# An output stage of seven products for all pairs, with every engine's operations placed on one clock

## The chip, the cores and the metric

The kernel runs on one core of one Trainium2 chip. Its engines are TensorE (PE), VectorE (DVE), ScalarE (ACT), GpSimd (POOL) and SyncE (SP), each with an instruction stream of its own that is worked off in order; they wait for each other by semaphores. The metric is the device time of one execution in microseconds (us). Before the change the median of three runs is 1524.33 us (1519.32 to 1524.88).

## The reference

One step of a hybrid decoder layer in fp32, for a prompt of 4096 tokens and 64 sample tokens with a width of 1024:

```python
h = _rmsnorm(x, g_pre)
z = h @ w_in
cb, cc, ch, cg, q, k, v, ag, mq, mg = _split_cols(z)
...
out_a = jax.nn.silu(cg) * cb * conv
...
out_b = jax.nn.silu(ag) * o_b
...
out_c = jax.nn.silu(mg) * o_c
y = jnp.concatenate([out_a, out_b, out_c], axis=-1) @ w_out
return x + _rmsnorm(y, g_post), new_conv, new_k, new_v
```

`out_a` is a gated short convolution (256 columns); `o_b` is attention over a sliding window of 128 keys with 8 query heads on 2 key heads (512 columns); `o_c` is attention of 4 heads over 256 memory tokens (256 columns). The softmax of the window has one more term per head, exp(sink - m), in its denominator, and m is the maximum over the scores and the sink.

## The kernel before

A product of two fp32 matrices is made of three matmuls on TensorE: both operands are split into a high and a low part (a cast and a subtraction), and high x high, low x high and high x low are added up in PSUM. A matrix of 2x2 blocks can be multiplied with seven block products instead of eight, at the price of sums of blocks ahead and combinations behind; the input projection does this for nearly all of its blocks (its matmuls are line 368, its evictions line 375).

The kernel has two parts. The input projection goes over blocks of 520 tokens in three phases and writes queries and keys (`qd`), values (`vd`) and the gated mix (`md`) to DRAM. Then comes the output stage, in 16 pairs (`c`) of two blocks of 128 tokens. For each pair it does two halves (`h`) of attention and one output projection, and TensorE's stream interleaves them: the small matmuls of a half stand between groups of output matmuls.

One half of attention consists of these steps: the window scores (`ws`, line 1333), copied to `sm` by ScalarE (line 1342) and masked by VectorE (`COPY_PREDICATED`); maximum, exponentials with their sums (line 1289), the sink's share (`wes`, line 1286, added to `wden`, line 1294), the multiplication by the reciprocal `wrd` (line 1297); transposes (`wt`), a copy to `wpt` (line 1307) and two selections by GpSimd (lines 1312 and 1315). Beside them the memory scores (`xs`, line 1355), exponentials (`xp`, line 1180), multiplication by the reciprocal `xrd` and 0.5 (line 1192, GpSimd, the "factors"), transposes (`xt`, line 1368) and a copy back (line 1369). Then come the products with the values (`wo`, lines 1390, 1396 and 1059) and the gates, which write into the pair's `place`.

The output projection of a pair is a product of 256 tokens x 1024 by 1024 x 1024. The first three pairs (`Block.run`, line 1639) do it plainly: 96 matmuls of 512 columns. The other thirteen (`Pair.run`, line 1750) use seven products for the k tiles 0 to 3 and plain matmuls for the k tiles 4 to 7: 90. The weights are kept on the chip in 16 split tiles `wo`, and the sums of weights (T1, T3, T4, T6, T7) are built during the first three pairs. The sums of the mix are made by GpSimd (line 1695), split by ScalarE and VectorE (lines 1678 and 1681); the products collect in four PSUM banks, `c12`, `c21`, `c11` and `c22`, and are combined by VectorE by way of the buffers `s3` and `s4` (lines 1770 to 1800). Each finished half row is multiplied by the gain (`gpost`), squared and summed (line 1753); from the sums comes a factor (`yst`, lines 1654 and 1655, the power on GpSimd), and the "residual" xr = y * factor + x (line 1660, 1024 columns) is stored.

The order of TensorE in the output stage is that of the program: a table of places (`what`, filled by `at`) calls the parts of attention and sums between the products. VectorE, ScalarE, GpSimd and SP are ordered by a scheduler, with a number of pinned instructions.

Of the kernel before, what the change touches and what calls it, by code (L numbers as in the profile page):

```python
# [52 lines left out]
def hybrid_layer(ctx: ExitStack, tc: tile.TileContext, a: dict):  # L53
# [23 lines left out]
    qd = tc.dram_tile([2, 7, P, NT], F32R, name="qd")  # L77
    vd = tc.dram_tile([P, NT], F32, name="vd")
# [22 lines left out]
    def open_phase(ph):  # L101
# [3 lines left out]
        if ph == 0:  # L105
            z = [z_pool(kept_z, f"z{n}") for n in range(4)]
            natp = own.enter_context(tc.tile_pool(name="nat", bufs=2))
            zp[2] = [*z, z_pool(own, "z4")]
            kept_z.z4 = zp[2][-1]
        elif ph == 1:  # L110
            zp[2].remove(kept_z.z4)
            zp[2][:0] = [z_pool(own, f"z{n}") for n in (5, 6, 7)]
        else:

            tp = [own.enter_context(tc.tile_pool(name=f"t2{n}", bufs=3)) for n in "ab"]
            z = [z_pool(own, n) for n in ("z8", "z9", "y0", "y1", "z10", "y2")]
            zp[2], zp[1] = [z[0], z[1], z[4]], [z[2], z[3], z[5]]
# [281 lines left out]
    def finish_parts(b, z, idx, second):  # L399

        z = flat(z)
        if idx == 0 and b == NBLK - 1:
            kl = temp("kl")
            S.copy(kl[:, :P], z[:, 2 * HW - P :])
            store(a["o_kp"], kl[:, :P])
        hi = temp(f"zh{b}_{idx}", second)[:, : 2 * HW].bitcast(F32R)
        S.copy(hi, z)  # L407
        lo = (temp("kl_")[:, : 2 * HW] if idx == 0 else z).bitcast(F32R)
# [315 lines left out]
    def third_start():  # L724
# [8 lines left out]
        negs = third["negs"] = keep.tile([P, 2, P], F32, name="negs")  # L733
        tc.keep_in_program_order(DMA.dma_start(sink, a["sinks"].partition_broadcast(P)))
        V.tensor_scalar(nsink, sink, -1.0, None, op0=ALU.mult)
        tc.keep_in_program_order(DMA.dma_start(negs, a["wmask"]))
        G.tensor_copy(wmask, negs)  # L737
# [6 lines left out]
        third["mem"] = mem_stack.enter_context(tc.tile_pool(name="mem", bufs=3, side="right"))  # L744
        tc.keep_in_program_order(DMA.dma_start(gmem, a["gmem"]))
# [142 lines left out]
    wo, wo_raw = [[None, None] for _ in range(KT)], {}  # L888

    def wo_load(j):  # L890
        h, k = divmod(j, KT)
        if 10 <= j < 14:

            if j % 2 == 0:
                third["raw"] = hxp.tile([P, KH, HW], F32, tag="hx", name=f"wor{j}").rearrange("p k n -> p (k n)")
            wo_raw[j] = third["raw"][:, 512 * (j % 2) : 512 * (j % 2) + 512]
        else:
            wo_raw[j] = third["work"].tile([P, 512], F32, tag="u", name=f"wor{j}")
        DMA.dma_start(wo_raw[j], a["w_out"][k][:, 512 * h : 512 * h + 512])

    def wo_split(j):
        h, k = divmod(j, KT)
        wo[k][h] = wa.tile([P, 2, 512], F32R, tag="w", name=f"wo{k}_{h}")
        w_split(wo[k][h], wo_raw.pop(j))
# [16 lines left out]
    def input_projection():  # L921
        for i, (ph, b, p) in enumerate(steps):
# [32 lines left out]
            if i > 0 and steps[i - 1][0] == 1 and steps[i - 1][1] == NBLK - 1:  # L955

                o = PRODUCTS[steps[i - 1][2]][0]
                for q in range(len(PHASES[2])):
# [5 lines left out]
                    else:  # L964
                        jobs.append(load)
                        pending.setdefault(i + 1, []).append(fill)
            if ph == 2 and b == last:
                for j in ((0, 1, 2), (3, 4), (5, 6, 7), (8, 9, 10, 11), (12, 13, 14, 15), (), ())[p]:
                    jobs.append(lambda j=j: wo_load(j))
                    pending.setdefault(i + (3 if j in (10, 11) else 2), []).append(lambda j=j: wo_split(j))  # L970
                if p == 1:
                    pending.setdefault(i + 1, []).append(gains_load)
                if p == 4:
                    jobs.append(blocks[0].split)
# [36 lines left out]
    def open_attention():  # L1011

        nonlocal ps, mixp, places, vp, bp, yp, wt, sums
# [9 lines left out]
        wt = att.enter_context(tc.tile_pool(name="wt", bufs=6))  # L1023
        places = {tag: att.enter_context(tc.tile_pool(name=tag, bufs=1 if tag == "p" else 2)) for tag in ("sm", "p", "yn", "pt", "pv")}
        sums = {tag: att.enter_context(tc.tile_pool(name=tag, bufs=1)) for tag in ("s3", "s4", "sum")}
        bp = {"k": att.enter_context(tc.tile_pool(name="keys", bufs=1)), "vT": att.enter_context(tc.tile_pool(name="vT", bufs=1))}
        mixp = att.enter_context(tc.tile_pool(name="mixp", bufs=1))
        late = att.enter_context(tc.tile_pool(name="late", bufs=1))
# [4 lines left out]
    ps = mixp = places = vp = bp = yp = wt = sums = None  # L1033
# [27 lines left out]
    left = []  # L1061

    def finish_block(queued=False):

        while left:
            left.pop(0)(queued)

    class Chunk:


        def __init__(self, c):
            self.c, self.rds, self.q, self.ks = c, {}, [None, None], [None, None]
# [3 lines left out]
        def load_values(self):  # L1076
            pool = third["pre"] if self.c == 0 or self.c % 2 else bp["vT"]
            self.vT = pool.tile([P, CT], F32, tag="vT", name=f"vT{self.c}")
            DMA.dma_start(self.vT, vd[:, self.ts])

        def load_all_keys(self):

            self.kst = third["pre"].tile([P, 4, P + CT], F32R, tag="k", name="kst0")
# [10 lines left out]
        def load_keys(self, i):  # L1094

            t = self.t0 + i * P
            pool = bp["k"] if i else third["pre"]
            self.ks[i] = pool.tile([P, 4, P + CT] if i == 0 else [P, 4, CT], F32R, tag="k", name=f"kst{self.c}_{i}")[:, :, :CT]
            self.fill_keys(G if self.c == 1 else DMA, self.ks[i], t - P, CT)
# [157 lines left out]
        def window_unit(self, i, kvh, steps):  # L1257
# [4 lines left out]
            for half in range(2):  # L1262
# [7 lines left out]
                V.copy_predicated(sm[:, 2 * half : 2 * half + 2, :], third["wmask"], third["negs"] if first else s3[:, :, 0:P])  # L1270
# [860 lines left out]
```

## Time and profile before

| | us |
|---|---|
| median of the runs | 1524.33 |
| span of the profiled execution | 1517.9 |
| input projection (0 to 928.70) | 928.70 |
| first three pairs | 114.10 |
| next twelve pairs, 35.4 each | 424.60 |
| last pair, with the sample tokens' | 40.80 |
| after the last matmul | 9.70 |

The profile is of one execution, whose span lies 6.4 us below the median. A row of groups gives the line, the engine, the operation, out<-in by the program's names, the shapes, the count, the busy time with the mean in ns of one, and the idle time of the engine ahead of them with what ended it. Matmuls overlap: a matmul of 512 columns is shown with about 395 ns, while the next one starts some 230 ns after it. So the price of a matmul is read from the starts in the timeline.

### The profile page before, as it was taken

Reading aid. Unit: us, or ns where it says so; the run is one execution under the profiler, and the core shown is the slowest. Engines: PE = TensorE matmul, PEld = TensorE weight load, DVE = VectorE, ACT = ScalarE, POOL = GpSimd, SP = SyncE. Lnnn points to the kernel's source line nnn. Section 1 sums busy time; section 2 is a strip of 40 time slices with the busy share of each in tenths; the row PEclk is TensorE's granted clock in tenths of the full one; section 3 lists DMA queues with packets and bytes.
Section 4 is the critical chain, followed back from the end, with each engine's and each line's share of the span. In section 5 each row is a group of like instructions: output and inputs, shape, how many; then the busy total and the mean of one; then the engine's idle time right before and its main releaser. Section 6 shows DMA issues by size and latency. Waiting matters only on the chain.

```text
span 1517.9 us, 30946 instructions
## 1 busy us (share of the span) xinstructions
PE 1500.6 (99%) x11497; PEld 1378.7 (91%) x11497; DVE 1199.3 (79%) x2089; ACT 842.7 (56%) x2066; POOL 392.7 (26%) x576
## 2 busy tenths in 40 slices
PE   9999999999999999999999999999999999999997
PEld 9999999999999999999999999788888788877875
DVE  6779888899988777897777768777877788878874
ACT  6676666475322222354454536666666666666652
POOL 0223222211300000000201301234455544455641
PEclk9999999999999999999999999999999999999999
DMA  9999999878855333578786697989755565666552
GB/s 258 157 265 221 289 294 271 264 246 298 211 183 183 128 116 125 180 235 292 227 265 238 208 307 252 282 238 238 201 168 157 160 164 162 176 174 169 153 201 70
DMA packets 217323, 319.71 MB, mean 211 GB/s; under 512 B 37398, under 2 KB 143382, under 8 KB 217142
## 3 DMA queue, kind: packets, MB, share of 16 engines
q1 hardware_dynamic: 196837, 273.54, 61.1%
q0 software_dynamic: 19616, 43.15, 10.5%
q8 instruction: 91, 1.49, 0.4%
q10 hardware_dynamic: 720, 1.05, 0.2%
q14 instruction: 59, 0.48, 0.1%
HBM read 208.50 MB, written 110.15 MB: 210 GB/s over the span
## 4 chain that ended last, share of the span: by engine, by line
PE 79%; DVE 8%; DMA 5%; ACT 4%; issue 2%; SPq 1%; POOL 0%; ACTq 0%; DVEq 0%; POOLq 0%
PE c L368 53%; PE y_c L1750 12%; PE y L1639 2%; PE ws L1333 2%; PE xt L1368 2%; ACT xp L1180 1%; DVE xr L1660 1%; DMA place<-in_xt 1%; PE wo L1059 1%; PE wo L1396 1%; DVE xmx L1169 1%; PE xs L1355 1%; DMA wr_3A<-in_w_in 1%; PE wt L1378 1%; DMA kst<-qd 1%
## 5 line engine op out<-in xcount | busy, mean ns | idle before, releaser
L375 DVE TENSOR_TENSOR z<-c,z 128x520 f32<-128x520 f32 (+1 forms) x308 | 194.3, 644 | 83.7 <-PE c L368 82.7
L1750 PE MATMUL y_c<-wo,pw 128*128 128x512 f32 (+1 forms) x636 | 158.9, 392 | 0.0
L1289 ACT ACTIVATE sm<-sm,wnm 128x128 f32<-128x128 f32 x256 | 99.4, 389 | 72.1 <-DVE wnm L1283 72.1
L1750 PEld LDWEIGHTS y_c<-wo,pw 128*128 128x128 f32 x636 | 114.0, 188 | 27.1 <-issue 3.7
L1192 POOL TENSOR_SCALAR xp<-xp,xrd 128x256 f32<-128x256 f32 x128 | 71.5, 575 | 191.2 <-DVE xrd L1186 186.7
L1180 ACT ACTIVATE xp<-xs,xnm 128x256 f32<-128x256 f32 x128 | 59.1, 473 | 31.5 <-DVE xnm L1170 22.9
L737 POOL CAST wmask<-negs 128x256 uint8<-128x256 f32 x1 | 1.2, 1162 | 266.7 <-DMA negs<-in_wmask 266.7
L1639 PE MATMUL y<-wo,mh 128*128 128x512 f32 x192 | 64.5, 398 | 0.2 <-ACT y L1648 0.2
L1312 POOL TENSOR_SCALAR_AFFINE_SELECT wpv<-wpt 128x512 f32<-128x512 f32 x62 | 56.8, 938 | 8.7 <-ACT wpt L1307 8.5
L1315 POOL TENSOR_SCALAR_AFFINE_SELECT wpt<-wpt 128x512 f32<-128x512 f32 x64 | 46.0, 737 | 38.6 <-ACT wpt L1307 38.2
L1333 PE MATMUL ws<-kst,q 128*128 128x256 f32 (+1 forms) x480 | 55.7, 297 | 0.0
L1343 DVE COPY_PREDICATED sm<-wmask,ws 128x512 f32<-128x512 uint8 x60 | 40.5, 729 | 19.0 <-ACT sm L1342 19.0
L1660 DVE SCALAR_TENSOR_TENSOR xr<-yn,yst,xr 128x1024 f32<-128x1024 f32 (+2 forms) x35 | 51.6, 1479 | 4.6 <-POOL yst L1655 4.5
L407 ACT CAST zh<-z 128x520 fp32r<-128x520 f32 x56 | 33.3, 624 | 35.3 <-DVE z L375 31.9
L276 ACT ACTIVATE nat<-nat 104x1024 f32<-104x1024 f32 x40 | 42.2, 1056 | 18.3 <-DMA nat<-in_x_p 18.3
L377 ACT COPY z<-c 128x520 f32<-128x520 f32 (+1 forms) x44 | 24.4, 554 | 49.3 <-PE c L368 45.0
L1333 PEld LDWEIGHTS ws<-kst,q 128*128 128x128 f32 (+1 forms) x480 | 46.4, 187 | 4.1
L1289 ACT ACTIVATION_READ_ACCUMULATOR sm<-sm,wnm 128x1 f32 x256 | 47.9, 187 | 0.0
L1297 DVE TENSOR_TENSOR sm<-sm,wrd 128x512 f32<-128x512 f32 x64 | 44.5, 695 | 1.1
L1750 PE MATMUL y_c<-wo,pc 128*128 128x512 f32 (+1 forms) x162 | 45.1, 400 | 0.0
L164 POOL DMA_DIRECT2D md<-th x48 | 26.2, 547 | 72.0 <-DVE th L425 59.5
L1639 PEld LDWEIGHTS y<-wo,mh 128*128 128x128 f32 x192 | 36.1, 188 | 8.9 <-issue 1.0
(1037 smaller groups left out, 5538.8 us busy)
## 6 DMA issues: line engine op xcount, KB each, us to landing
q<-qd SPq DMA_DIRECT2D x168, 128.0 KB
xr<-in_x_p SPq DMA_DIRECT2D x32, 512.0 KB
nat<-in_x_p SPq DMA_DIRECT2D x39, 416.0 KB
o_yp<-xr SPq DMA_DIRECT2D x31, 512.0 KB
kst<-qd SPq DMA_DIRECT2D x112, 128.0 KB
md<-th POOLq DMA_DIRECT2D x48, 260.0 KB, 6.4
qd<-zh SPq DMA_DIRECT2D x48, 260.0 KB
qd<-z SPq DMA_DIRECT2D x48, 260.0 KB
```

The costliest lines, as they stand in the source:

```text
L368: TE.matmul(bank[:, :HW], l, r, start=first and i == 0, stop=last and i == 3 * KH - 1)
L375: add = lambda dst, other: V.tensor_tensor(dst, c, other, op=ALU.add)
L1180: S.activation(p[:, i, :], s[:, i, :], AF.Exp, bias=nm[:, i : i + 1], scale=SCALE, accum_out=den[:, i : i + 1])
L1192: G.tensor_scalar(p[:, i, :], p[:, i, :], self.rds[h][:, i : i + 1], 0.5, op0=ALU.mult, op1=ALU.mult)
L1289: S.activation(sm[:, hh, :], sm[:, hh, :], AF.Exp, bias=nm[:, hh : hh + 1], scale=SCALE, accum_out=den[:, hh : hh + 1])
L1297: V.tensor_tensor(sm, sm, rd.unsqueeze(2).to_broadcast([P, 4, P]), op=ALU.mult)
L1312: G.affine_select(pv.rearrange("p (h q) -> p h q", h=4), p3, pattern=[[0, 4], [-1, P]], compare_op=ALU.is_gt, fill=0.0, base=0, channel_mu ...
L1315: G.affine_select(p3, p3, pattern=[[0, 4], [1, P]], compare_op=ALU.is_ge, fill=0.0, base=0, channel_multiplier=-1)
L1333: TE.matmul(out(kvh, col, bank), q(kvh, col, bank)[r], k(kvh, part)[r], start=first, stop=True, skip_group_check=not first, **place)
L1639: TE.matmul(acc, self.hl[l][:, k], wo[k][p][:, r], start=k + i == 0, stop=k + i == KT + 1)
L1660: x = V.scalar_tensor_tensor(self.xr[:m, cs], yn[:m, cs], st[:m, 3:4], self.xr[:m, cs], op0=ALU.mult, op1=ALU.add)
L1750: TE.matmul(acc, a[:, l, k], w[:, r, cs], start=first, stop=k == len(ws) - 1 and i == 2, skip_group_check=not new)
```

## The change

All 16 pairs now use seven products for the whole of the projection: the eight k tiles are put into two groups of four, (0, 1, 4, 5) and (2, 3, 6, 7), and each product has four k tiles, so a pair has 7 x 4 x 3 = 84 matmuls. The last of the products of the last pair stays in two quarters.

The weights follow. The sums T1, T3, T4, T6, T7 and the plain b11 are built and split by GpSimd during phase 1 of the input projection (21 tiles; 41 loads, 41 sums or differences, 21 casts, 42 stores to DRAM), and b22 and most of b11 late in phase 2. The fourth k tile of six operands has no place on the chip and is loaded again for each pair (`STREAMED`, six DMAs of 512 KB a pair on SP).

In the output stage all five engines now follow one table: each operation of attention, projection, loads and stores has a place in units of a period of 34.0 per pair, and the five streams are written in the order of the places. Besides, the factors move from GpSimd to ScalarE (their 0.5 goes into the copy behind the transposes); the sink becomes a 129th column of `sm`, so that the exponentials' sums hold it and `wes` and its addition go; the squares and gains of two half rows read PSUM, without a copy ahead; keys are kept in a ring of three blocks, which halves their loads; the raw projections of the sample tokens are kept in DRAM (`zd`).

```diff
+    G0, G1 = (0, 1, 4, 5), (2, 3, 6, 7)
+    STREAMED = (("T3", 3), ("T4", 3), ("b11", 3), ("T1", 3), ("T6", 3), ("T7", 3))
...
+    def out_sum(o, j):
+        x, y = out_raw.pop((o, j))
+        if o in WALKED:
+            G.tensor_tensor(x, x, y, op=ALU.subtract if o in ("T3", "T4") else ALU.add)
+        hi, lo = y.bitcast(F32R), x.bitcast(F32R)
+        G.tensor_copy(hi, x)
+        G.tensor_tensor(lo, x, f(hi), op=ALU.subtract)
+        G.dma_start(f(td[o, j][:, 0]), f(hi))
+        G.dma_start(f(td[o, j][:, 1]), f(lo))
...
+        def window_sink(self, i, kvh):
+            S.copy(self.sms[kvh][:, :, P:], third["nsink"][:, 4 * kvh : 4 * kvh + 4].unsqueeze(2))
...
+        def memory_factors(self, h, p):
+            for i in range(CT // P):
+                S.mul(p[:, i, :], p[:, i, :], self.rds[h][:, i : i + 1])
...
+    PERIOD = 34.0
...
+        SUMS = {"rows0": ((1, 0), (0, 0), ALU.add), "rows1": ((1, 1), (0, 1), ALU.add), "diag": ((1, 0), (0, 1), ALU.add),
+                "down0": ((1, 1), (1, 0), ALU.subtract), "down1": ((0, 0), (0, 1), ALU.subtract)}
...
+        def direct(self, n, p, bank):
+            S.activation(self.half(n, p), self.acc[bank], AF.Square, scale=float(D) ** -0.5, accum_out=self.st[n][:, p : p + 1])
...
+    ORDER = (("M1", "c12", "a11", "T3", True), ("M3", "c12", "rows0", "b22", False), ("M2", "c21", "a22", "T4", True),
+             ("M4", "c21", "rows1", "b11", False), ("M5", "c11", "diag", "T1", True), ("M7", "c11", "down1", "T7", False),
+             ("M6", "c22", "down0", "T6", True))
...
+                "s4": lambda: p.combine("s4", "s3", "c21", ALU.add), "y00": lambda: p.combine((0, 0), "s4", "c12", ALU.subtract),
```

**TensorE, early in the ninth pair (`y8`), around the transposes and scores of half 19.** `xt` and `ws` are the transposes and window scores of that half, `wo9` its products with the values, `y8_...` the output products. Before:

```order
L1750 MATMUL y8_c21_15831<-wo2_0_11644,pr8_15804 128x512 x3
L1750 MATMUL y8_c21_15831<-wo3_0_11688,pr8_15804 128x512 x3
L1750 MATMUL y8_c12_15830<-wo4_1_11863,pw0_8_15884 128x512 x3
...
L1750 MATMUL y8_c12_15830<-wo6_1_11882,pw0_8_15884 128x512 x3
L1750 MATMUL y8_c12_15830<-wo7_1_11885,pw0_8_15884 128x512 x3
L1368 MATMUL xt9_0_15932<-ident_63,xp9_0_15789 128x128 x8
L1333 MATMUL ws19_0_15942<-kst9_1_15633,q9_1_15638 128x256 x4
L1333 MATMUL ws19_1_15943<-kst9_1_15633,q9_1_15638 128x256 x4
...
L1390 MATMUL wo9_0_15962<-wpv18_0_15852,vt8_1_15378 64x256
...
L1059 MATMUL wo9_0_15962<-xp9_0_15789,mkv_8464 64x128 x8
L1750 MATMUL y8_c21_15831<-wo4_0_11691,pw1_8_15905 128x512 x3
```

After (`woT4` with `a228` is M2, `wob22` with `rows08` M3, `wob11` with `rows18` M4):

```order
L1660 MATMUL y8_c21_15947<-woT4_0_11938,a228_15878 128x512 x3
L1660 MATMUL y8_c21_15947<-woT4_1_11940,a228_15878 128x512 x3
L1660 MATMUL y8_c12_15894<-wob22_0_11847,rows08_15888 128x512 x3
L1660 MATMUL y8_c21_15947<-woT4_2_11973,a228_15878 128x512 x3
...
L1660 MATMUL y8_c12_15894<-wob22_3_11902,rows08_15888 128x512 x3
L1660 MATMUL y8_c21_15947<-woT4_3_15876,a228_15878 128x512 x3
L1431 MATMUL xt9_0_16050<-ident_63,xp9_0_15943 128x128 x8
L1366 MATMUL ws19_0_16064<-ring_10053,q9_1_15958 128x256 x4
L1366 MATMUL ws19_1_16065<-ring_10053,q9_1_15958 128x256 x4
...
L1660 MATMUL y8_c21_15947<-wob11_0_12015,rows18_15995 128x512 x3
```

Before, the products of `wo2_0` with `pr8` (the later M4) stood ahead of the transposes, the products with the values followed the scores, and the next output matmuls went on in `c21` with the window's part `pw1`. Now M2 into `c21` ends directly ahead of the transposes, and M4, into the same bank, begins directly behind the scores; the products with the values come behind it.

**VectorE at the same place.** `s4` is the combination that reads `c21`, `xr` the residuals of the pair before, `sm18` the shares of half 18. Before:

```order
L1770 TENSOR_TENSOR yn7_1_15363<-y7_c22_15668,s3_7_15366 128x512
...
L1654 TENSOR_SCALAR yst7_1_15365<-yst7_1_15365 128x1
L1776 TENSOR_TENSOR yn7_1_15363<-yn7_1_15363,gpost_11647 128x512
L1787 TENSOR_TENSOR s4_8_15829<-s3_8_15828,y8_c21_15831 128x512
L1681 TENSOR_TENSOR pw0_8_15884<-place_159,pw0_8_15884 128x512
L1790 TENSOR_TENSOR yn8_0_15824<-s4_8_15829,y8_c12_15830 128x512
L1660 SCALAR_TENSOR_TENSOR xr15_14977<-yn7_1_15363,yst7_1_15365,xr15_14977 128x1024
L1681 TENSOR_TENSOR pw1_8_15905<-place_159,pw1_8_15905 128x512
L1793 TENSOR_TENSOR s3_8_15828<-s4_8_15829,y8_c21_15831 128x512
L1681 TENSOR_TENSOR pd8_15915<-diag8_15916,pd8_15915 128x256
L1681 TENSOR_TENSOR pc8_15926<-yn8_1_15825,pc8_15926 128x512
L1343 COPY_PREDICATED sm19_0_15979<-wmask_8468,ws19_0_15942 128x512
```

After:

```order
L1401 RECIPROCAL wrd18_0_15970<-wden18_0_15863 128x4
L1403 TENSOR_TENSOR sm18_0_15822<-sm18_0_15822,wrd18_0_15970 128x4x128
L1599 TENSOR_SCALAR yst7_0_15588<-yst7_0_15588 128x1
L1685 TENSOR_TENSOR yn7_0_15587<-yn7_0_15587,gpost_12206 128x512
L1213 RECIPROCAL xrd9_1_15992<-xden9_1_15951 128x2
L1604 SCALAR_TENSOR_TENSOR xr15_15892<-yn7_1_15603,yst7_1_15604,xr15_15892 128x1024
L1647 TENSOR_TENSOR diag8_15979<-rdiag8_15874,diag8_15979 128x512
L1647 TENSOR_TENSOR rows18_15995<-rrows18_15913,rows18_15995 128x512
L1604 SCALAR_TENSOR_TENSOR xr14_15890<-yn7_0_15587,yst7_0_15588,xr14_15890 128x1024
L1695 TENSOR_TENSOR s4_8_16088<-s3_8_15938,y8_c21_15947 128x512
L1678 TENSOR_TENSOR yn8_0_16043<-y8_c12_15894,gpost_12206 128x512
L1695 TENSOR_TENSOR yn8_0_16043<-s4_8_16088,y8_c12_15894 128x512
```

The residual `xr14` of the pair before now stands directly ahead of `s4_8`, with a share, a gain, the other residual and two lows in front of it; before, `s4_8` stood behind a gain, and the nearer residual came after it.

**ScalarE around the exponentials of the memory scores, in the eighth pair.** Before (the factors are on GpSimd, line 1192):

```order
L1678 CAST pa8_15650<-place_159 128x256 x2
L1759 COPY yn7_1_15363<-y7_c21_15369 128x512
L1180 ACTIVATE xp8_1_15589,xden8_2_15590<-xs8_1_15572,xnm8_2_15582 128x256 x2
L1180 ACTIVATE xp8_1_15589,xden8_3_15593<-xs8_1_15572,xnm8_3_15586 128x256 x2
L1307 COPY wpt17_0_15623<-wt17_15614 128x512
L1307 COPY wpt17_1_15628<-wt17_15614 128x512
L1753 ACTIVATE s4_7_15367,yst7_1_15365<-yn7_1_15363 128x512
L1369 COPY xp8_1_15589<-xt8_1_15669 128x1024
```

After:

```order
L1207 ACTIVATE xp8_0_15488,xden8_0_15489<-xs8_0_15449,xnm8_0_15480 128x256 x2
L1207 ACTIVATE xp8_0_15488,xden8_1_15496<-xs8_0_15449,xnm8_1_15476 128x256 x2
L1643 CAST diag7_15524<-rdiag7_15419 128x512
L1643 CAST rows17_15539<-rrows17_15458 128x512
L1424 ACTIVATE xp8_0_15488<-xp8_0_15488,xrd8_1_15536 128x256 x2
L1424 ACTIVATE xp8_0_15488<-xp8_0_15488,xrd8_0_15513 128x256 x2
L1455 ACTIVATE vt8_0_15470<-vtp8_15472 128x128
L1455 ACTIVATE vt8_1_15471<-vtp8_15472 128x128
```

The four factors (`xp8_0<-xp8_0,xrd8`) stand on ScalarE behind two casts of the next products' parts and ahead of the copies `vt`; the copy `yn7_1<-y7_c21` is no longer there.

More of the change, by code (lines that the diff above doesn't have):

```diff
@@ L1011, in open_attention @@
     def open_attention():
-        nonlocal ps, mixp, places, vp, bp, yp, wt, sums
+        nonlocal ps, mixp, places, vp, yp, wt, sums
         own.close()
@@ L2011, in hybrid_layer @@
[L2011 to L2024 removed]
+    ctx.enter_context(tc.manual_schedule(engines={mybir.EngineType.PE, mybir.EngineType.DVE, mybir.EngineType.SP,
+                                                  mybir.EngineType.Activation, mybir.EngineType.Pool}))
@@ L2025, in hybrid_layer @@
+    extra("tokens", sample_tokens)
+    for bh in range(2):
+        plan_sample_memory(bh)
+    plan_sample_window()
+    for o in ("T4", "T3"):
+        extra(f"sample {o}", lambda o=o: out_load(o, 3))
+    plan_sample_out()
+    plan_end()
+    for _, _, fn in sorted(plan, key=lambda item: item[:2]):
+        fn()
     att.close()
```

1200 lines of the change are left out of this document (583 added, 617 removed), and 20 rows, old and new, of tables (EXTRA, FIRST_HALVES, HALF).

## The prediction

> **What bounds the kernel now.** I read the page first, then the busy time by stage, then what TensorE waits for, and last one pair of the output stage instruction by instruction. The page says that TensorE is busy 99% of the span and carries 79% of the chain that ended last:
>
> ```profile
> span 1517.9 us, 30946 instructions
> ...
> PE 1500.6 (99%) x11497; PEld 1378.7 (91%) x11497; DVE 1199.3 (79%) x2089; ACT 842.7 (56%) x2066; POOL 392.7 (26%) x576
> ...
> PE 79%; DVE 8%; DMA 5%; ACT 4%; issue 2%; SPq 1%; POOL 0%; ACTq 0%; DVEq 0%; POOLq 0%
> ```
>
> By stage (columns: length; busy time and count of TensorE, of its weight load, of VectorE, ScalarE and GpSimd; granted clock; DMA share; GB/s) the rows are the input projection, the first three pairs, the next twelve pairs, the last pair, and the tail:
>
> ```profile
> 0.00:928.70 928.70, 924.64 (x7676) 916.45 (x7677) 745.68 (x1060) 466.43 (x797) 133.88 (x213) 1.00 0.76 227
> 928.70:1042.80 114.10, 112.94 (x752) 92.03 (x751) 88.06 (x207) 74.58 (x254) 37.97 (x59) 1.00 0.94 265
> 1042.80:1467.40 424.60, 422.52 (x2825) 339.75 (x2824) 337.47 (x758) 284.51 (x968) 212.46 (x290) 1.00 0.61 171
> 1467.40:1508.20 40.80, 40.49 (x248) 30.50 (x246) 24.49 (x60) 16.67 (x45) 7.38 (x13) 1.00 0.42 134
> 1508.20:1517.90 9.70, 0.03 (x1) 0.00 (x0) 3.61 (x7) 0.51 (x2) 1.01 (x2) 0.69 0.27 81
> ```
>
> TensorE's idle time is 4.1 us of 928.7, 1.2 of 114.1, 2.1 of 424.6 and 9.7 in the tail, at a granted clock of 1.00 throughout. Its waits are small; the longest single one that the view names in the output stage is this (total, times, longest):
>
> ```profile
> PE xt L1368 <- POOL xp L1192: 0.6, 1, 0.6
> ```
>
> So in the output stage the time is the sum of matmuls, one behind the other. A removed matmul is a saved one as long as the other engines still deliver in time, and they have room: one steady pair (the fifth of the twelve) reads, in the same columns,
>
> ```profile
> 1188.55:1223.96 35.41, 35.28 (x237) 28.43 (x237) 28.42 (x65) 23.93 (x83) 17.43 (x24) 1.00 0.61 166
> ```
>
> which leaves VectorE 7.0 us, ScalarE 11.5 us and GpSimd 18.0 us of 35.41 free.
>
> **The matmuls removed.** By the order of the program, output matmuls of 512 columns go from 96 (first three pairs) or 90 (the others) to 84 a pair, and the last pair loses 12 of 256 columns: 3x12 + 12x6 + 6 = 114 of 512 columns. The price is in TensorE's timeline of that pair (start, length, names, count):
>
> ```profile
> 1188.55 3.08 PE L1750 MATMUL y_c<-wo,pr 128*128 128x512 f32 x12
> 1191.46 2.99 PE L1750 MATMUL y_c<-wo,pw 128*128 128x512 f32 x12
> 1194.30 1.03 PE L1368 MATMUL xt<-ident,xp 128*128 128x128 f32 x8
> 1195.09 1.85 PE L1333 MATMUL ws<-kst,q 128*128 128x256 f32 x16
> 1196.87 0.43 PE L1390 MATMUL wo<-wpv,vt 64*64 64x256 f32 x2
> ...
> 1199.35 1.66 PE L1750 MATMUL y_c<-wo,pw 128*128 128x512 f32 x6
> 1200.84 1.54 PE L1750 MATMUL y_c<-wtT,pd 128*128 128x512 f32 x6
> 1202.22 1.11 PE L1355 MATMUL xs<-mk,q 128*128 128x256 f32 x8
> ...
> 1206.82 2.89 PE L1750 MATMUL y_c<-wo,pw 128*128 128x512 f32 x12
> 1209.55 1.03 PE L1368 MATMUL xt<-ident,xp 128*128 128x128 f32 x8
> ```
>
> From start to start, twelve matmuls take 2.91, 2.84 and 2.73 us: 0.2275 to 0.2425 each. I take 0.235: 114 x 0.235 = **-26.8 us** (-25.9 to -27.6). The Trainium skill (TensorE: Matmul & The Clock Gate, Wait — 56ns, not 53.3ns?) puts back-to-back matmuls at N / 2.4 GHz plus about 2.5 ns, 215.7 ns at 512 columns; by it the term would be -24.6. The rows here are 5 to 12% longer than that, and the rows decide.
>
> **More group starts.** Six matmuls that follow small ones take 1.49 us (1199.35 to 1200.84), the six behind them 1.38: a start costs 0.11. By the order, a steady pair now has nine places at which output matmuls follow other matmuls, and seven before: 2 x 0.11 x 16 = **+3.5 us** (0 to 7).
>
> **ScalarE, VectorE, GpSimd in the new pair.** From the same pair (busy, mean ns of one):
>
> ```profile
> L1192 POOL TENSOR_SCALAR xp<-xp,xrd 128x256 f32<-128x256 f32 x8 | 4.5, 576 | 10.3 <-DVE xrd L1186 10.3
> L1678 ACT CAST pa<-place 128x256 fp32r<-128x256 f32 x2 | 0.7, 396 | 0.0
> L1678 ACT CAST pc<-yn 128x512 fp32r<-128x512 f32 x1 | 0.6, 621 | 0.0
> L1286 ACT ACTIVATE wes<-wes 128x4 f32<-128x4 f32 x4 | 0.7, 189 | 0.0
> L1759 ACT COPY yn<-y_c 128x512 f32<-128x512 f32 x2 | 1.2, 588 | 3.3 <-PE y_c L1750 3.3
> L1695 POOL TENSOR_TENSOR yn<-mix 128x512 f32<-128x512 f32 x1 | 1.5, 1452 | 0.0
> L1695 POOL TENSOR_TENSOR sum<-place 128x256 f32<-128x256 f32 x2 | 1.5, 736 | 7.4 <-ACT sm L1289 5.1 <-DVE wes L1285 2.4
> L1776 POOL TENSOR_TENSOR yn<-yn,gpost 128x512 f32<-128x512 f32 x1 | 1.3, 1276 | 0.3 <-ACT s L1753 0.3
> ```
>
> The eight factor multiplications of a pair leave GpSimd (-4.5) for ScalarE. No trace shows that operation on ScalarE; the cast of the same 128x256 is the nearest row, 0.396, and the bounds are 0.19 (a 4-column operation) and 0.62 (a 512-column one): +3.2 us (1.5 to 5.0). ScalarE also loses four wes (-0.7) and two copies of y_c (-1.2; the squares now read PSUM), gains four 4-column sink copies (+0.7) and some 768 cast columns (+0.9, at 0.621 for 512): 23.9 + 2.9 = 26.8 of 34. GpSimd trades four 256-wide sums (2.9) for four 512-wide ones (5.8) and gives a gain back to VectorE (-1.3): 17.4 - 4.5 + 2.9 - 1.3 = 14.5. VectorE keeps about 28 less the wes and wden operations. All three fit beside some 34 us of matmuls, so what is left is the order: each waits in line.
>
> **The new tight place.** The order of the places puts one VectorE addition, s4, directly in front of TensorE: it must be done before the products of b11 write the same bank (called M4 here), and s4 itself waits for the products of T4 (M2). Between M2's end and M4 stand one set of transposes and one of scores, 1196.87 - 1194.30 = 2.57 us by the timeline. Directly ahead of s4 VectorE has the residual of the pair before; behind s4 wait a gain, y00 and the next half's mask. The rows:
>
> ```profile
> L1660 DVE SCALAR_TENSOR_TENSOR xr<-yn,yst,xr 128x1024 f32<-128x1024 f32 x2 | 3.4, 1704 | 0.0
> L1787 DVE TENSOR_TENSOR s<-s,y_c 128x512 f32<-128x512 f32 x1 | 0.7, 675 | 0.0
> L1766 DVE TENSOR_TENSOR yn<-yn,gpost 128x512 f32<-128x512 f32 x2 | 1.6, 798 | 1.4 <-ACT s L1753 1.4
> L1297 DVE TENSOR_TENSOR sm<-sm,wrd 128x512 f32<-128x512 f32 x4 | 2.8, 689 | 0.1
> ```
>
> If the residual begins as M2 ends, 1.70 + 0.68 = 2.38 us stand against 2.57: 0.2 us of slack, and VectorE arrives there behind a queue that holds two shares (0.69 each), a gain (0.80), the other residual (1.70) and two lows (as wide as a share; 0.69 each is my estimate). A second place is the transposes of the even half: they wait for the last factor on ScalarE, which stands behind the xexp and two casts there; on GpSimd four factors took 2.3 us, on ScalarE they should take about 1.6. I take 0.12 us per pair for both places together, **+2 us** (0 to 16, one us a pair).
>
> **Streamed weights.** Six tiles of 512 KB are now loaded again in each pair on SP's queue, among the queries, keys and stores. Each is issued behind the last products of its tile's predecessor, and SP waits there; queued behind it are the next half's queries and keys. The key loads halve (eight of 128 KB to 64 KB). The pair now moves 166 GB/s x 35.41 us = 5.9 MB at a share of 0.61; with 3.1 more and 0.5 less it is 8.5 MB in 34 us, 250 GB/s. The first three pairs ran at 265 GB/s and a share of 0.94 with TensorE busy 112.94 of 114.10, so the volume fits; I take **0** (0 to 16).
>
> **Stage start and input projection.** Before, the output stage began with twelve output matmuls (2.7 us by the price above), which covered the last evictions; the first scores now stand there and need them. The eviction of 512 columns is 0.69 (row below), and the first products wait for a softmax. I take **+2 us** (0 to 5). In phase 1 GpSimd gets 41 sums of 512 columns (1.452 each: 59.5 us) and 21 casts, where it had nearly nothing, and 41 loads. The phase has VectorE busy 745.68 of 928.70. Its most frequent group takes the same time where GpSimd is busy 78 of 290 us (first rows) and where it is busy 15 of 320:
>
> ```profile
> 40.00:330.00 290.00, 288.06 (x2416) 287.06 (x2415) 240.65 (x314) 184.60 (x333) 78.44 (x126) 1.00 0.96 256
> 380.00:700.00 320.00, 320.00 (x2698) 319.90 (x2697) 265.93 (x373) 108.85 (x142) 15.10 (x16) 1.00 0.56 179
> ...
> L375 DVE TENSOR_TENSOR z<-c,z 128x520 f32<-128x520 f32 x77 | 52.2, 691 | 16.5 <-PE c L368 16.4
> ...
> L375 DVE TENSOR_TENSOR z<-c,z 128x520 f32<-128x520 f32 x108 | 73.6, 693 | 34.2 <-PE c L368 34.1
> ```
>
> I take **0** (0 to 5). The tail after the last matmul keeps its operations (add, square, factor, residual, store): **0** (-1 to 2).
>
> **The sum.** -26.8 + 3.5 + 2 + 0 + 2 + 0 + 0 = -19.3, on the span of this execution: 1517.9 - 19.3 = 1498.6. The median of the runs, 1524.3, lies 6.4 above that span (the lowest run 1.4); I carry the 6.4 over: **1505 us**.
>
> **The rivals.** (1) Nothing is lost: the starts cost nothing, the chains hold. -26.8 gives 1497.5, say 1498. For it: TensorE was idle only 2.1 us in twelve pairs. Against it: s4's slack of 0.2 us.
>
> (2) The pair becomes bound by a chain instead of by TensorE: s4 or the factors are late by one us in each of 16 pairs, in place of the 0.12: +14, 1519, which is no change. For it: 79% of 34 us on ScalarE and over 80% on VectorE, in a fixed order. Late weight tiles, one us a pair, give the same 1519.
>
> (3) Slower: VectorE is held up beside GpSimd's longer sums on the way to s4. Place: the row of down0, 512 columns on GpSimd, falls in the order beside factor, residual and lows of VectorE. The multiplication by the gain took 798 ns above and 1.15 us where GpSimd worked beside it (first two rows below). Price, in place of the 2 us above: if the whole 1.45 us of one sum is lost per pair, 1.45 - 0.2 of slack = 1.25, x 16 = 20: 1523, no change; if two sums or selects meet the chain, 2.90 - 0.2 = 2.7, x 16 = 43: 1546. It decides from 2 + 19.3 + 7.6 = 28.9 us lost, 1.8 a pair. The Trainium skill (SBUF — State Buffer, Terms) has the port pair of VectorE and GpSimd as an exclusive lock, held for a whole instruction, so that the loser is blocked; by it this rival would be likely. The timeline here speaks against a full lock: a residual of two SBUF inputs took 1.57 us inside 2.20 us of selects (last two rows).
>
> ```profile
> 1188.06 0.72 POOL L1695 TENSOR_TENSOR diag<-mix 128x256 f32<-128x256 f32 x1
> 1188.18 1.15 DVE L1776 TENSOR_TENSOR yn<-yn,gpost 128x512 f32<-128x512 f32 x1
> ...
> 1191.09 2.20 POOL L1312 TENSOR_SCALAR_AFFINE_SELECT wpv<-wpt 128x512 f32<-128x512 f32 x2
> 1191.23 1.57 DVE L1660 SCALAR_TENSOR_TENSOR xr<-yn,yst,xr 128x1024 f32<-128x1024 f32 x1
> ```
>
> That the matmuls are not removed is excluded by the order.
>
> **How the numbers follow.** 0.5% (7.6 us) is about what a measurement of this kernel can tell from no change. Forecast and its neighbourhood (1500 to 1515) 0.58; rival 1, 0.12; rival 2, 0.20, its loss spread from 0.7 to 1.8 us a pair about the one of its price (under 0.9 it is still faster, over 1.8 slower): 0.03 faster, 0.15 same, 0.02 slower; rival 3, 0.10, of which 0.03 same (one sum) and 0.07 slower. Faster by over 0.5%: 0.58 + 0.12 + 0.03 = 0.73. Same: 0.15 + 0.03 = 0.18. Slower: 0.02 + 0.07 = 0.09. The range leaves out part of rival 1 below and the end of rival 3 above: 1496 to 1525.
>
> **What the profile after would show.** A steady pair of 34.0 to 34.3 us with TensorE busy to within 0.3 us, nine starts, 0.4 us factors on ScalarE, 14 to 15 us of GpSimd. The waits by TensorE are the test: no line of M4 on VectorE's s4 or of the transposes on ScalarE's factors beyond 2 us in all. I am wrong if the pair is over 35 us, if VectorE's residual and lows are longer than 1.70 and 0.69, if products wait for a weight tile's transfer, or if the input projection ends later than 930 us.

## The result and the profile after

The changed kernel takes 1503.82 us (median of 4 runs, 1501.46 to 1505.70) against 1524.41 (4 runs, 1519.32 to 1524.88): a ratio of 0.9877, 95% interval 0.9852 to 0.9902. Two later controls, the same kernel beside new runs of the kernel before, gave 0.9898 (0.9873 to 0.9922) and 0.9906 (0.9885 to 0.9927). The forecast was 1505.

The page of the changed kernel:

```profile
span 1501.0 us, 31210 instructions
...
PE 1479.7 (99%) x11377; PEld 1356.0 (90%) x11377; DVE 1225.0 (82%) x1984; ACT 888.7 (59%) x2163; POOL 467.8 (31%) x573
```

By stage (the input projection; the start of the output stage with the first pair; fourteen pairs; the last pair; the tail), in the columns of before:

```profile
0.00:930.30 930.30, 924.39 (x7676) 915.83 (x7676) 764.96 (x1059) 460.96 (x789) 250.90 (x323) 1.00 0.83 251
930.30:978.03 47.73, 43.47 (x269) 32.96 (x267) 33.96 (x67) 33.56 (x112) 14.74 (x16) 0.96 1.00 315
978.03:1455.52 477.49, 476.60 (x3220) 381.01 (x3219) 399.57 (x801) 380.76 (x1229) 189.52 (x218) 1.00 0.84 255
1455.52:1491.90 36.38, 35.10 (x218) 26.18 (x216) 22.47 (x50) 12.60 (x32) 10.77 (x14) 1.00 0.80 266
1491.90:1501.00 9.10, 0.13 (x2) 0.00 (x0) 4.02 (x9) 0.82 (x4) 1.92 (x3) 0.63 0.30 95
```

One steady pair, with all of its length busy on TensorE:

```profile
1148.56:1182.67 34.11, 34.11 (x232) 27.33 (x230) 28.54 (x58) 27.22 (x88) 13.49 (x15) 1.00 0.82 246
```

The transposes of the values, which come once a pair, start 34.11 us apart, thirteen times without a deviation in the second decimal; before, in the steady pairs, they started 35.33 to 35.69 apart. So what the view shows of TensorE's losses is at the edges: its idle time is 4.3 us in the first stretch of the output stage and 1.3 in the last pair, and 0.9 in the fourteen pairs between. The waits that the view names are these (total, times, longest):

```profile
PE c L369 <- DVE lo_2B L360: 1.7, 1, 1.7
...
PE y_c L1660 <- DMA woT<-tdT: 1.3, 1, 1.3
PE y_c L1660 <- DVE a L1647: 1.0, 1, 1.0
PE y_c L1660 <- ACT s L1698: 1.0, 1, 1.0
PE c L369 <- DVE lo_0B L360: 0.9, 1, 0.9
```

The first and the last are in the input projection, the two of 1.0 us at the start of the output stage, the 1.3 us in the last pair (a tile of T1). The page's order of engines did not turn: TensorE is still the one at 99%.

### The profile page after: what moved, and what is told of

It reads as the page before. It is cut to its first block, busy times and chain, and to the rows that moved or that the text cites. A ratio compares the mean times of both kernels' runs of the same rounds, so it can differ in the third digit from the quotient of the medians.

```text
span 1501.0 us, 31210 instructions
## 1 busy us (share of the span) xinstructions
PE 1479.7 (99%) x11377; PEld 1356.0 (90%) x11377; DVE 1225.0 (82%) x1984; ACT 888.7 (59%) x2163; POOL 467.8 (31%) x573
## 5 line engine op out<-in xcount | busy, mean ns | idle before, releaser
L1397 ACT ACTIVATE sm<-sm,wnm 128x129 f32<-128x129 f32 x240 | 93.2, 391 | 32.3 <-DVE wnm L1390 32.2
L1660 PE MATMUL y_c<-wob,rows 128*128 128x512 f32 x384 | 106.9, 408 | 1.0 <-ACT s L1698 1.0
L1660 PE MATMUL y_c<-woT,a 128*128 128x512 f32 x384 | 103.3, 399 | 1.0 <-DVE a L1647 1.0
L1660 PE MATMUL y_c<-woT,down 128*128 128x512 f32 (+1 forms) x396 | 102.4, 400 | 0.5 <-DVE yn L1678 0.4
L1660 PEld LDWEIGHTS y_c<-wob,rows 128*128 128x128 f32 x384 | 69.2, 190 | 18.7 <-issue 2.8
L1660 PEld LDWEIGHTS y_c<-woT,down 128*128 128x128 f32 x396 | 69.2, 188 | 18.5 <-issue 2.6
L1660 PEld LDWEIGHTS y_c<-woT,a 128*128 128x128 f32 x384 | 70.1, 189 | 15.7 <-DVE a L1647 1.4
L1366 PE MATMUL ws<-ring,q 128*128 128x256 f32 (+1 forms) x480 | 56.0, 298 | 1.3 <-ACT wpt L1340 0.8
L1424 ACT ACTIVATE xp<-xp,xrd 128x256 f32<-128x256 f32 x120 | 51.3, 505 | 0.0
L1660 PE MATMUL y_c<-woT,diag 128*128 128x512 f32 x192 | 47.8, 395 | 1.3 <-DMA woT<-tdT 1.3
L165 POOL DMA_DIRECT2D md<-th x48 | 26.3, 549 | 65.4 <-DVE th L428 59.9
```

Of the source, the lines that this page charges most:

```text
L1366: TE.matmul(out(kvh, col, bank), q(kvh, col, bank)[r], k(kvh, part)[r], start=first, stop=True, skip_group_check=not first, **place)
L1397: S.activation(sm[:, hh, :], sm[:, hh, :], AF.Exp, bias=nm[:, hh : hh + 1], scale=SCALE, accum_out=den[:, hh : hh + 1])
L1424: S.mul(p[:, i, :], p[:, i, :], self.rds[h][:, i : i + 1])
L1660: TE.matmul(self.acc[bank], self.parts[name][:, l, j], wo[o][j][:, r, cs], start=new and j + i == 0, stop=j == 3 and i == 2, skip_group_ch ...
```

## The experiments

The theory (A): TensorE's matmuls alone set a pair, the change saves their time, and everything else only has to be there in time. Its rivals are that the moved operations or the new order are the gain themselves (B), and that a chain on another engine is at its edge (the second and third rival of the prediction).

### Six matmuls put back

```diff
                 self.acc[bank] = psum("z", f"y{self.c}_{bank}")[:, cs]
+                if name in ("diag", "down0"):
+                    for i, (l, r) in enumerate(((0, 0), (1, 0), (0, 1))):
+                        TE.matmul(self.acc[bank], self.parts[name][:, l, j], wo[o][j][:, r, cs], start=i == 0, stop=i == 2)
```

> The changed kernel with six output matmuls of 512 columns more in each of the first 15 pairs (the first three of T1 and of T6 are done twice, the second time into the cleared bank), so 90 a pair as before. Theory A (TensorE's matmuls alone set the pair, 34.11 us): 6 x 0.2275 to 0.2425 = 1.37 to 1.46 a pair, a steady pair of 35.5 to 35.6 us, and 15 x 1.4 = 21 us more, 1525 against 1504: the whole gain is given back. Theory B (the gain came as much from the new order and the moved operations): TensorE would have idle time to fill, the pair grows by less than 0.7 and the kernel stays under 1515.

Measured: 1525.11 us, ratio 1.0025 (1.0010 to 1.0039). A pair:

```profile
1161.00:1196.38 35.38, 35.38 (x238) 28.48 (x237) 28.58 (x58) 27.25 (x88) 13.50 (x15) 1.00 0.76 238
```

The gain is gone, and TensorE is still busy all the time. Theory A holds, B falls. The pair grew by 35.38 - 34.11 = 1.27 us, but the six did not cost 0.212 each. The timelines show where it grew; first the changed kernel, then this one, around the second three:

```profile
1167.83 3.02 PE L1660 MATMUL y_c<-woT,down 128*128 128x512 f32 x12
1170.69 1.12 PE L1431 MATMUL xt<-ident,xp 128*128 128x128 f32 x8
1171.57 1.19 PE L1366 MATMUL ws<-ring,q 128*128 128x256 f32 x8
```

```profile
1180.89 0.94 PE L1661 MATMUL y_c<-woT,down 128*128 128x512 f32 x3
1181.68 2.91 PE L1663 MATMUL y_c<-woT,down 128*128 128x512 f32 x12
1184.43 1.04 PE L1431 MATMUL xt<-ident,xp 128*128 128x128 f32 x8
1185.22 1.51 PE L1366 MATMUL ws<-ring,q 128*128 128x256 f32 x10
```

From start to start the output matmuls went from 2.86 to 3.54 us, 0.68 for three, and the three of T1 cost the same. The transposes behind them went from 0.88 to 0.79. So the six cost 1.27 + 0.09 = 1.36 us, 0.227 each, which is the low end of the starts in the timeline of before. The 0.09 is a wait that no view names, because it stands between the overlapping matmuls of one group: in the changed kernel the last factor on ScalarE ends at 1171.21, when the transposes have begun, and two of the eight are held back.

```profile
1169.51 1.70 ACT L1424 ACTIVATE xp<-xp,xrd 128x256 f32<-128x256 f32 x4
```

With six matmuls more ahead of them the factors are there in time.

### The factors put back on GpSimd

```diff
-                S.mul(p[:, i, :], p[:, i, :], self.rds[h][:, i : i + 1])
+                G.tensor_scalar(p[:, i, :], p[:, i, :], self.rds[h][:, i : i + 1], 1.0, op0=ALU.mult, op1=ALU.mult)
```

> The changed kernel with the eight factor multiplications of a pair put back on GpSimd. Theory A (everything beside TensorE only has to fit): GpSimd goes from 13.5 to some 18 us of 34.11, the four factors ahead of the even transposes end about 0.5 us later than on ScalarE, where they ended 1.3 us before the transposes; steady pair 34.1, time 1503 to 1505. Rival (the move was needed for the pair to hold): transposes or selections late by 0.5 us or more, pair 34.6 or more, time 1511 or more.

Measured: 1556.0 us, ratio 1.0235 (1.0207 to 1.0263). Pairs of 36.9 and 38.4 us mostly take turns. The rival held, and by more than it said. TensorE's waits, and then GpSimd and VectorE in one pair (start, length):

```profile
PE xt L1431 <- POOL xp L1424: 28.7, 27, 1.6
```

```profile
1097.07 1.27 DVE L1604 SCALAR_TENSOR_TENSOR xr<-yn,yst,xr 128x1024 f32<-128x1024 f32 x1
...
1098.25 0.69 DVE L1647 TENSOR_TENSOR diag<-rdiag,diag 128x512 fp32r<-128x512 f32 x1
1098.85 0.69 DVE L1647 TENSOR_TENSOR rows<-rrows,rows 128x512 fp32r<-128x512 f32 x1
1099.45 1.28 DVE L1604 SCALAR_TENSOR_TENSOR xr<-yn,yst,xr 128x1024 f32<-128x1024 f32 x1
```

```profile
1097.48 3.52 POOL L1424 TENSOR_SCALAR xp<-xp,xrd 128x256 f32<-128x256 f32 x1
...
1100.98 1.38 POOL L1424 TENSOR_SCALAR xp<-xp,xrd 128x256 f32<-128x256 f32 x3
```

The four factors are not slowed evenly. The first begins 0.41 us after a residual and takes 3.52 us: VectorE's residual, two lows and the second residual, which read two tensors of SBUF each, follow each other without a gap, and the factor ends 0.27 us after the last of them. The three behind it take 1.38 together, 0.47 each, though VectorE works on, on operations that read PSUM. VectorE's own durations are those that it has without the factors (1.27 and 0.68). The even transposes behind them are 1.6 us late. Of the 2.8 us that the shorter pairs grow, the waits of the view are 2.1 in each (1.6 and 0.5). The longer pairs have the same waits, and a lower granted clock behind them, 0.96 x 38.43 = 36.9:

```profile
1055.20:1093.63 38.43, 36.22 (x231) 28.73 (x230) 28.46 (x58) 24.07 (x80) 20.27 (x23) 0.96 0.75 223
1093.65:1130.55 36.90, 34.69 (x232) 27.30 (x230) 28.47 (x58) 24.15 (x80) 20.29 (x23) 1.00 0.81 239
```

### One and three operations ahead of s4

```diff
-                "s4": lambda: p.combine("s4", "s3", "c21", ALU.add),
+                "s4": lambda: [p.combine("s4", "s3", "s3", ALU.add) for _ in range(3)] + [p.combine("s4", "s3", "c21", ALU.add)],
```

(range(1) in the first of the two.)

> The changed kernel with one more VectorE addition of 512 columns (0.68 us) directly ahead of s4 in every pair. By the trace of the changed kernel s4 ends 1.49 us before the matmul that needs its bank: no change, pair 34.11. By the prediction's slack of 0.2 us: 0.48 a pair, 34.6, time 7 us longer.

> The same with three additions (2.04 us). By the slack of 1.49 us: 0.55 late, pair 34.66, time 8 us longer, and the wait stands in TensorE's waits as y_c on s4 of VectorE. By the prediction's 0.2 us: 1.84 a pair, 35.95, time 28 us longer. If TensorE can put other work in its place: 34.11.

The changed kernel without an edit shows the place as follows: residual, transposes, s4, scores, and the first matmul of M4.

```profile
1154.37 1.27 DVE L1604 SCALAR_TENSOR_TENSOR xr<-yn,yst,xr 128x1024 f32<-128x1024 f32 x1
...
1155.15 1.03 PE L1431 MATMUL xt<-ident,xp 128*128 128x128 f32 x8
...
1155.57 0.68 DVE L1695 TENSOR_TENSOR s<-s,y_c 128x512 f32<-128x512 f32 x1
...
1155.94 1.86 PE L1366 MATMUL ws<-ring,q 128*128 128x256 f32 x16
...
1157.74 1.67 PE L1660 MATMUL y_c<-wob,rows 128*128 128x512 f32 x6
```

s4 ends at 1156.25, M4 starts at 1157.74. One addition: pairs of 34.11 (one run, 1507.45 us). Three: pairs of 35.53 (one run, 1529.93 us), and the wait has the name that was expected:

```profile
PE y_c L1660 <- DVE s L1695: 19.5, 15, 1.4
```

So one more operation of 0.69 us fits and three that took 2.76 do not, as the trace of the changed kernel says; the slack is not 0.2. Three cost 1.42 instead of 0.55 because they were longer than 0.68: they ran beside GpSimd's selections, and both slowed down (0.69, 1.00 and 1.00 instead of 0.68; two selections 3.09, which take 1.23 where VectorE leaves them alone).

```profile
1169.08 3.09 POOL L1341 TENSOR_SCALAR_AFFINE_SELECT wpv<-wpt 128x512 f32<-128x512 f32 x2 [2.29 <-PE y_c L1660]
...
1169.95 2.76 DVE L1695 TENSOR_TENSOR s<-s 128x512 f32<-128x512 f32 x3
```

2.76 - 1.49 = 1.27 of the 1.42 us.

### A control

> The changed kernel itself, unedited, on the chip of the next three. Both theories: a steady pair of 34.11 us and a time some 1.2% under the kernel before; it is there to be compared with.

Measured: 1506.53 us, ratio 0.9898 (0.9873 to 0.9922), pairs of 34.11.

### The streams doubled

```diff
-                put(place, lambda o=o: out_load(o, 3))
+                put(place, lambda o=o: (out_load(o, 3), DMA.dma_start(f(again[o]), f(td[o, 3]))))
```

> The changed kernel with a second transfer of 512 KB, DRAM to DRAM, behind each streamed weight load: six more a pair, from 250 to some 340 GB/s if the pair stays at 34.1. Theory A (TensorE alone sets the pair; the streams of the change have room to spare): DMA share from 0.83 to at most 1.0; if the transfers just fit, the pair stays at 34.1 to 34.3. Rival (transfers are nearly the bound): 28 us of transfers a pair by the share of 0.83 plus 9 to 11 for 3.1 MB make 37 to 39 us, TensorE waits for weight tiles, queries or keys, and the pair becomes 36 to 39, the kernel 1535 to 1580.

Measured: 1547.97 us, ratio 1.0170 (1.0141 to 1.0200), pairs of 35.4 to 40.8 us. The rival held. A stretch of 37 us, and the largest wait:

```profile
1100.00:1137.00 37.00, 36.19 (x234) 28.57 (x232) 28.70 (x57) 27.32 (x88) 13.55 (x15) 0.95 0.91 310
```

```profile
PE ws L1367 <- DMA q<-qd: 18.9, 29, 3.0
```

It is mostly the queries that come late; weight tiles cost 2.0 us, once. SP issues the queries in one queue with the doubled transfers and waits there for these (26.3 us in 32 waits between 1000 and 1400), so this run does not tell whether the rate of the transfers or the place in this queue is the bound. The room beside the streams of the change is smaller than six transfers of this kind; how many would fit was not tried, and a transfer from DRAM to DRAM need not cost what one to SBUF costs.

### The order of three engines left to the scheduler

```diff
-    ctx.enter_context(tc.manual_schedule(engines={mybir.EngineType.PE, mybir.EngineType.DVE, mybir.EngineType.SP,
-                                                  mybir.EngineType.Activation, mybir.EngineType.Pool}))
+    ctx.enter_context(tc.manual_schedule(engines={mybir.EngineType.PE, mybir.EngineType.SP}))
```

> The changed kernel with only TensorE's and SP's streams in the order of the table; VectorE, ScalarE and GpSimd are ordered by the scheduler again, with the same operations. Theory A (TensorE alone sets the pair as long as the others fit): they fit by volume (28.5, 27.2 and 13.5 us of 34.11), so the pair is 34.1 to 35 and the time at most 1518. Rival (it is the placing on one clock that lets them fit, as the factors on GpSimd showed: a volume that fits and a pair of 36.9 to 38.4): TensorE waits for late operations in most pairs, 1 to 4 us a pair, time 1520 to 1570.

Measured: 1543.31 us, ratio 1.0144 (1.0107 to 1.0181), pairs of 35.3 to 37.1 us. The rival held: the same operations, in the same volume, and TensorE waits.

```profile
PE wt L1442 <- DVE sm L1403: 12.2, 10, 1.6
PE y_c L1660 <- ACT a L1643: 4.5, 1, 4.5
PE xt L1431 <- ACT xp L1424: 3.2, 13, 0.2
```

So theory A needs its second half said aloud: the matmuls set the pair only because the order of the other engines was placed so that nothing is late. With the same 84 matmuls and another order the kernel is slower than before.

### No sums in phase 1

```diff
-            G.tensor_tensor(x, x, y, op=ALU.subtract if o in ("T3", "T4") else ALU.add)
+            pass
...
-        G.tensor_tensor(lo, x, f(hi), op=ALU.subtract)
+        G.tensor_copy(lo, x)
```

> The changed kernel without the sums of weights in phase 1: GpSimd only casts the first summand into both parts and stores them, so that the output is not that of the reference. Theory (two-input operations of GpSimd and VectorE hold each other up): the wait of TensorE for lo_2B at the place where one sum took 2.35 us and the low part 2.31 instead of 1.30 and 1.24, 2.0 us of the input projection, goes, and every low part of 1040 columns takes 1.24. Rival (lo_2B is late for another reason, a transfer or ScalarE): the wait of about 2 us stays. The second wait, at the start of phase 2, stays by both.

The changed kernel shows, where TensorE waits 1.7 us for lo_2B (gap between two matmuls: 2.0):

```profile
424.93 1.23 DVE L349 TENSOR_TENSOR x_2T<-place,x_2B 128x1040 f32<-128x1040 f32 x1
424.94 2.35 POOL L916 TENSOR_TENSOR os0T<-os0T,os1T 128x512 fp32r<-128x512 f32 x1
...
426.07 2.31 DVE L360 TENSOR_TENSOR lo_2B<-x_2B,hi_2B 128x1040 fp32r<-128x1040 f32 x1
```

Without the sums (one run, 1499.47 us) that wait is not there any more, and lo_2B takes what the other lows take:

```profile
L360 DVE TENSOR_TENSOR lo_2B<-x_2B,hi_2B 128x1040 fp32r<-128x1040 f32 x2 | 2.5, 1240 | 0.4 <-ACT hi_2B L359 0.4
```

The wait for lo_0B at the start of phase 2 stays. Theory held, with two remarks. The three lines above are a chain: GpSimd's operation (the low part of a sum of weights) began 0.01 us after VectorE's sum x_2T and ended 1.14 after it, lo_2B began inside GpSimd's and ended 1.09 after it. And not every low part takes 1.24: of 154, 13 take over 1.3 us in the changed kernel (up to 2.94), five without the sums, three in the kernel before. The projection ended at 928.2.

### The start of the output stage, and the sums moved

```diff
-"first4": -3.467
+"first4": -15.0
...
-            put(place, jobs[name])
+            put(0.3 if c == 0 and name == "s3c" else place, jobs[name])
```

and, in the second kernel, also

```diff
-    out_sums_at = [(1, b, p) for b in range(1, NBLK - 1) for p in ((5, 6) if b < 4 else (1, 2, 3, 4, 5))]
+    out_sums_at = [(1, b, p) for b in range(1, NBLK - 1) for p in ((), (), (2,), (1, 2, 3, 4, 5))[min(b, 3)]]
```

> The changed kernel with two operations of the first pair placed earlier: the low part of a22 on VectorE (ahead of a maximum instead of behind four operations) and the copy s3 on ScalarE (ahead of eight exponentials). They ended the two waits of 1.0 us at the start of the output stage, behind which twelve matmuls started 0.427 us apart instead of 0.23. Theory A (the gaps bring the clock down): waits and slow matmuls both go, 2.0 + 2.2 us, of which the softmax of half 3, whose shares ended 1.1 us before TensorE came to their transposes, gives back up to 3; the total is 1 to 3 us shorter. Theory C (the start is bound by the first softmax, TensorE only waits elsewhere): the same 34.11, a wait of 2 to 3 us of the transposes wt on sm, total within 1 us.

> The same, and the 21 sums of weights of phase 1 moved: one in block 2, five in each of the blocks 3 to 6, instead of two in each of 1 to 3 and five in 4 to 6. If the wait of 2.0 us is a chance meeting of one sum with lo_2B, it goes, unless another meeting takes its place: 0 to 2 us shorter than e9_start. If the start of phase 2 waits for the transfers of weights that the sums' stores delay, it becomes longer by 1 to 2 us.

> The changed kernel itself again, to be compared with the two: 1.0 to 1.3% under the kernel before, a steady pair of 34.11.

Measured against the kernel before: 0.9898 (0.9882 to 0.9915), 0.9917 (0.9898 to 0.9937) and, for the control, 0.9906 (0.9885 to 0.9927). No difference among the three can be told. In the traces the two waits of 1.0 us went and one of 2.4 or 2.6 came, of the transposes `wt` behind the first softmax:

```profile
PE wt L1442 <- ACT diag L1643: 2.4, 1, 2.4
```

From the start of the projection's last matmul to the third pair's values it is 47.79 and 46.48 us against 47.85 in the control, but these are not alike: in the first and in the control the granted clock was 0.50 for 3.4 us of the way, in the second it stayed at 1.00. The earlier control, whose clock stayed at 1.00 there too, took 46.29. Like with like, 47.79 stands against 47.85 and 46.48 against 46.29: the move gained nothing. The start is bound by the first softmax (theory C); what is moved there only moves the wait. In the second kernel TensorE waited for another low part instead (lo_4B, 2.4 us, in place of lo_2B).

## Why the prediction was right, point by point

**The bound and the sign: right.** The output stage is a sum of matmuls, before and after; putting six of them back in each pair took the gain away.

**The sum: 1505 against 1503.82, but by terms that made up for each other.** The output stage became 17.90 us shorter (579.50 to 561.60). In it:

- *The matmuls removed* (-26.8, -25.9 to -27.6): at 0.227 each 114 are -25.9, the end of the range. The page of the Trainium skill that the prediction weighed gave -24.6 (TensorE: Matmul & The Clock Gate, Wait — 56ns, not 53.3ns?: 215.7 ns); the 0.227 of the added matmuls is 5% above it. The starts in the timeline were the right rows, and 0.235 was 0.008 too much.
- *Group starts* (+3.5): the prediction counted seven places before and nine after; the timelines have six and nine. A steady pair went from 35.38 (424.60 in twelve), of which 0.17 were idle, to 34.11, of which 0.09 are the factors' wait. 35.21 - 6 x 0.227 = 33.85 and 34.02 - 33.85 = 0.17 a pair, 2.7 in 16, is what is left for three more starts; no run has them alone.
- *The tight place at s4 and the factors* (+2, 0 to 16): 0 at s4, 0.09 us in each of thirteen pairs at the factors, +1.2. The step of the prediction that failed is "0.2 us of slack" at s4: it let the residual begin as M2 ends, where it begins 0.78 us ahead of the transposes, and took 1.70 us for it, the mean of two that ran beside GpSimd's selections and sums (1.57 and 1.84), where it takes 1.27 now. The slack is 1.49. The place that is tight is the other one. And "four factors took 2.3 us on GpSimd, 1.6 on ScalarE" missed what the move is worth in this order: 2.8 to 4.3 us a pair.
- *Streamed weights* (0): right, with a share of 0.82 as against 0.61. In the last pair one tile was 1.3 us late; the prediction had named a wait of products for a tile as a sign of being wrong.
- *Stage start* (+2, 0 to 5): larger. TensorE was idle 4.3 us from 930.30 to 978.03, and its granted clock was 0.50 for 3.4 us of it, which cost 1.7; that part is chance, as the last section shows. In the whole output stage its idle time grew from 3.55 to 6.43 us, so that -25.9 + 2.7 + 1.2 + 1.7 + 2.9 = -17.4 stands against the measured -17.90; 0.5 us stay without a name.

Outside it, *the input projection* (0, 0 to 5) ended 1.6 us later; two waits are new, 1.7 us by the meeting of GpSimd's sums with VectorE and 0.9 at the start of phase 2. This profile flatters the term. In the ten profiles of kernels with the same instructions in the projection it ended between 930.2 and 937.7, always later than the 928.6 of before and than the 930 that the prediction named as a sign of being wrong. Without the sums of weights it ended at 928.2. The term was too small; by how much stays open, since equal projections differ by 7.5 us and there is one profile each of before and without the sums. *The tail* was 0.6 us shorter.

**The span and the median.** I carried 6.4 us from span to median. The profiled execution of before was the run of 1519.32, 5 us under its median; that of after was 1502.76, 1 us under. The spans differ by 16.9, the medians by 20.6. A span of 1498.6 was forecast and 1501.0 measured, so the agreement of the medians to 1.2 us is partly luck.

**Rival 1** (nothing is lost) is what the steady pairs came near to: its terms make a pair of 33.97, those of the forecast 34.31, and it is 34.11. **Rival 2** (a chain in place of TensorE) did not happen, beyond the 0.09 us of the factors; three operations ahead of s4 show where it begins. **Rival 3** (VectorE held up beside GpSimd) did not happen in the steady pair: there the second residual begins first and keeps its 1.27 us, and the selection that meets it takes 1.45 instead of 0.64, for which nobody waits. The mechanism is there all the same: in phase 1 it cost 2.0 us once, and with the factors on GpSimd it costs the whole gain and more. What the prediction held against it was misread. Its row of selections, 2.20 us, is two of them:

```profile
1191.09 0.63 POOL L1312 TENSOR_SCALAR_AFFINE_SELECT wpv<-wpt 128x512 f32<-128x512 f32 x1
...
1191.68 1.61 POOL L1312 TENSOR_SCALAR_AFFINE_SELECT wpv<-wpt 128x512 f32<-128x512 f32 x1
```

The residual of 1.57 us began inside the first and ended at 1192.80, later than its 1.27; the second began inside the residual and ended at 1193.29, 0.49 after it, in 1.61 instead of 0.63. Each was held by the one ahead of it. The rule of the Trainium skill (SBUF — State Buffer, Terms: the loser is blocked) fits these rows, the factor of 3.52 us and the chain to lo_2B.

## What to carry to other kernels

When one engine is busy all the time, a removed instruction there is worth its marginal price. Adding a few of the same measures it, but read it where they were added: the pair's growth of 1.27 us was short of the price by a wait of 0.09 that went at the same time. The rest of a large change is worth nothing by itself, and can still be what the gain depends on. That the other engines fit by volume (13.5 to 28.5 of 34.11 us) says little: with the same volumes and another order, or with one kind of operation on another engine, the kernel was 1.4 to 2.4% slower than before. Take a duration for a chain from a place where no neighbour works beside it, or give both.

## What the runs showed of the hardware

**GpSimd and VectorE.** Which one is held up depends on the operations and, in the rows read here, on which began first. A factor on GpSimd (one SBUF tensor) that began behind a residual of VectorE took 3.52 us instead of 0.47, until four operations of two SBUF tensors each were done; these kept their time. A residual that began inside a selection took 1.57 instead of 1.27. Where two begin together either can lose: a residual of before that began 0.01 us ahead of a sum took 1.84, and the sum its 0.75. A mean hides this: four factors take 4.88 us, and three of them are not slowed at all. Other pairs take no notice of each other: an eviction from PSUM (691 and 693 ns before, 692 after), and a maximum over `sm` (0.68) inside a sum of GpSimd (1.28).

**The granted clock at short gaps.** After the two waits of 1.0 us at the start of the output stage the granted clock fell to half for 3.4 us; nine matmuls run in this stretch (not twelve, as an expectation above says), up to 0.427 us apart.

```profile
941.38:944.79 3.41, 3.41 (x9) 2.63 (x9) 2.49 (x5) 3.36 (x12) 1.82 (x2) 0.50 0.94 344
```

The same two waits stand in eight more profiles. In two (three operations ahead of s4, the last control) the clock fell too, in six it stayed at 1.00. One wait of 2.4 us brought it to 0.50 in one of the two kernels with the moved start, and one of 2.6 us left it at 1.00 in the other; with the factors on GpSimd the same wait of 1.5 us brought it down in six of fourteen pairs, at 1.5 us a time. What decides is not settled by these runs; a wait of 1 to 3 us can cost another 1.5 to 1.7 behind it.
